# A hidden block's ScalarE chain put off by one product, weight splits held back by a landing time, and idle products at the start, in a two-layer streaming encoder on one core

## The chip, the cores and the metric

The kernel runs on one core of a Trainium2 chip. The core has five engines with instruction queues of their own: TensorE (PE, matrix products, with its weight loads shown as PEld), VectorE (DVE), ScalarE (ACT), GpSimd (POOL) and SyncE (SP, which here issues nearly all transfers). The metric is the device time of one execution in microseconds (us), as the median of several runs.

## What is computed

One step of an encoder with two layers, on 1024 rows of a prompt and 32 rows of a running stream, 1024 features each. Cut to what matters here (rmsnorm is a root mean square norm over the features):

```
for i in (0, 1):
    sh1, sc1, gt1, sh2, sc2, gt2 = split(silu(c) @ w_ada[i] + b_ada[i], 6)
    h = rmsnorm(x, g_norm[i, 0]) * (1 + sc1) + sh1
    mix = sgu_mixer(h)  if i == 0 else  pool_mixer(h)
    x = x + gt1 * rmsnorm(mix, g_norm[i, 1])
    h = rmsnorm(x, g_norm[i, 2]) * (1 + sc2) + sh2
    f = square(relu(h @ w_up[i])) @ w_down[i]        # 1024 -> 4096 -> 1024
    x = x + gt2 * rmsnorm(f, g_norm[i, 3])
```

The mixer of layer 0 is a gated MLP (1024 to 2 x 2048, a 128 x 128 mix of positions, back to 1024); that of layer 1 takes trailing means of 2, 4, 8 and 16 rows and a small product per group. All of it is float32, and the last rows of some intermediate results are outputs too.

## The kernel before

**Tiles.** Activations lie transposed in SBUF, features on the 128 partitions in 8 blocks, rows along the free axis, in three tiles: rows 0 to 383, 384 to 767, and the last 256 with the 32 rows of the running stream.

**Products.** A float32 product is made of three products of a shorter type: each operand is split into a high part (ScalarE writes a rounded copy, names with h: wh, hh, fh) and a low part (VectorE subtracts, names with l: wl, hl, fl), and TensorE adds high times high, low times high and high times low into one PSUM bank. PSUM banks come from three rings: pu (2 banks), pd (3) and pm (3); a ring's next tile waits until the readers of the tile that had the bank are done.

**Weights.** All weights are streamed in one fixed list. `issue` (L463) sends the next load, 512 KB, from SP's queue as soon as one of the few raw buffers is free. `stream_step` takes the next load of the list and issues its split: on ScalarE the high part (L542 for a whole piece, L500 for a part of a quad), on VectorE the low part. The conditioning (w_ada) comes through the same list; VectorE works on it in products of a vector (the tiles aa, line 80 as all operations of its helper) and reduces them (part).

**The order of the work.** The kernel's text is a program in which two clocks are kept by hand while it is written out, `time["pe"]` and `time["dve"]`. `weave` (L765) is called behind each group of products and puts in what fits: a step of the weight stream, if `stream_waits` (L757) doesn't hold it back, and steps of other work (fillers: norms, gates, statistics). A scheduler of the framework then orders the instructions of each engine once more; only the front, in which the order is written out by hand, is kept as it stands (`tc.manual_schedule()`). Each engine executes its instructions in the order that results, so an instruction that waits holds up all behind it on its engine.

**The front** transposes the input rows (xT, L695), makes the first norm (its factor is spread over the partitions by three products with a matrix of ones, pb_h, L850), and the first six conditioning vectors on PE (ada, L583; ScalarE copies the result to adas, L595; two transposes adat, L600, bring it into columns). Then come the products of the gate's v half (pv, L1138), whose operands hh and hl need the norm and the conditioning.

**The channel MLP** runs in passes over its 4096 hidden features; the list `passes` counts them from n = 0. In 14 of them, n = 2 to 8 in layer 0 and n = 15 to 21 in layer 1, tiles 0 and 1 are taken together as a pair (`pair_item`, L1568). A pass has 512 hidden features, in four blocks j, for each tile. Two halves `up(0)` and `up(1)` make two blocks each, in seven products instead of eight, by combinations of the four quarters of the weights (A1, S31, S24, A22, from `quads`) and of the two tiles (combo). Each is a `quad_product` of 12 matmuls of 128 x 128 by 384 columns (L1604 to L1606), in this order of accumulators: pa, pb, pa, pb, pa, pc, pa. The bank of pa goes on accumulating, so ScalarE copies it to SBUF (L1610) at each stage that is used: a1, a2, a3, and pb once, b1. VectorE adds the hidden blocks r12 = a2 + pb, r22 = a3 + b1 and r11 = a1 + pc; r21 is pa at its end. The next product into a bank waits for its copy.

`keep` makes of each hidden block relu (L1578), square (L1579) and a split into a high part (L1326, ScalarE) and a low part (line 80, VectorE). Of a pass's eight blocks the first five go to tiles fh and fl, two to spare tiles that the profile shows as combo_R, and the last to fx. `down` then multiplies them by w_down, 8 blocks of features for each of the two tiles (accumulators pg, three banks, L1066 to L1068), and VectorE adds each to the residual's tile (acc). For the first blocks of the second tile the kernel puts the products of the last hidden block behind the others.

In `up` as it stands, each `keep` is called at once: for instance behind the third use of pa

```
a3 = copy(pa, f"a3{name}")
keep(0, j + 1, add(a3, b1, f"r22{name}"))
weave()
```

Of the kernel before, what the change touches and what calls it, by code (L numbers as in the profile page):

```python
# [11 lines left out]
AF = mybir.ActivationFunctionType  # L12
# [3 lines left out]
P = 128  # L16
# [19 lines left out]
def tile_stream_encoder_step(  # L36
# [26 lines left out]
    act = nc.scalar.activation  # L63
    mm = nc.tensor.matmul
# [3 lines left out]
    time = {"pe": 0.0, "dve": 0.0}  # L68
# [43 lines left out]
    ident = const.tile([P, P], F32, name="ident")  # L112
# [30 lines left out]
    def ps_ms(name):  # L143
        return psum.tile([P, 512], F32, tag="pm", bufs=3, name=name)

    def t_m(name):
        return work.tile([P, 384], F32, tag="m", bufs=3, name=name)
# [21 lines left out]
    one = t_hid("h", "one", F32)  # L169
# [270 lines left out]
            wpos[("up", key[1], key[2] // 2, x)] = wpos[key]  # L440
    raws = {}
    loads = {}
    state = {"issued": 0, "next": 0, "raw": 0, "used": 0, "folds": 0}
    deferred = []

    def in_raw(k):
# [13 lines left out]
    def issue():  # L460
        while state["issued"] < len(stream):
            k = state["issued"]
            kind, key, ap, shape = stream[k]  # L463
            if in_raw(k):
                if state["raw"] == RAW_SLOTS:
                    return
                state["raw"] += 1
                r = t_raw(f"raw{k}")
            elif kind == "x":
                r = x_rows[min(key // 3, NT - 1)]  # L470
                r = r[:, key % 3] if key < 6 else r
            else:
                r = w_tile(f"raw{k}")
            if kind == "x" and key < 6:
                i = nc.sync.dma_start(r, ap.rearrange("t (k n) -> t k n", n=P))
            elif kind == "x":
                for j in range(ap.shape[0] // 32):
                    for a in range(4):
                        i = nc.sync.dma_start(
                            r[32 * a : 32 * a + 32, 4 * (key - 6) + j],  # L480
                            ap[32 * j : 32 * j + 32].rearrange("s (k a m) -> s a k m", a=4, m=32)[:, a],
                        )
            else:
                i = nc.sync.dma_start(r.rearrange("p (a b) -> p a b", a=shape[0]), ap)
            raws[k] = r
            loads[key] = i.ins
            state["issued"] += 1

# [268 lines left out]
    def stream_waits():  # L757

        kind, key = stream[state["next"]][:2]
        if kind in ("w", "one", "two"):  # L760
            return bool(fillers) and wpos[key] > state["used"] + 5 and time["dve"] > time["pe"] + 1.0
        return kind in ("ada", "wide") and time["dve"] > time["pe"] + 0.5
# [52 lines left out]
    def weave(streams=1):  # L815
        if streams:
            n = 0
            run_deferred()
            while n < streams and stream_ready() and not stream_waits():
                stream_step()  # L820
                n += 1
        while time["dve"] < time["pe"] - slack[0] and fillers:
            if not pull():
                break
# [287 lines left out]
    def stream_to(kind, key):  # L1112
        k = max(i for i, s in enumerate(stream) if s[0] == kind and s[1] == key)
        while state["next"] <= k:
            stream_step()
        run_deferred()
# [38 lines left out]
    def fold():  # L1155
        pe_folds.pop(0)()
# [4 lines left out]
    def lo():  # L1161
        late_lo.popleft()()

    def row(h):

        next(h)
        next(h)

    with tc.manual_schedule():
        load_vectors(nc.scalar, 2, slice(0, 2))  # L1170
        issue()
        load_vectors(nc.gpsimd, 0, slice(0, 1))
        load_vectors(nc.gpsimd, 1, slice(0, 1))
        load_vectors(nc.gpsimd, 2, slice(2, 4))
        bring(AF.Silu)
        stream_to("x", 0)
        turn_conditions()
        stream_to("x", 2)
        bring(AF.Sqrt)
        next(h0)  # L1180
        next(h0)
        stream_to("ada", (0, 4, 0))
        turn_vectors()
        stream_to("ada", (0, 4, 1))
        next(h0)
        statistics(h0)
        fold()
        next(h0)
        stream_to("ada", (0, 0, 1))
        fold()  # L1190
        stream_to("w", ("v", 0, 0))
        next(h0)
        late_hi.pop()()
        next(h0)
        lo()
        early_mm((0, 1, 2), 0)
        stream_to("x", 5)
        next(h1)
        turn()
        next(h1)  # L1200
        stream_to("ada", (0, 5, 1))
        turn()
        fold()
        next(h1)
        statistics(h1)
        turn()
        early_ps.extend(ps_up(f"pv0_{b}") for b in (3, 4))
        next(h1)
        row(h1)
        stream_to("ada", (0, 1, 1))  # L1210
        next(h0)
        early_mm((3,), 0)
        fold()
        early_mm((4,), 0)
        for q in range(1, 4):
            stream_to("w", ("v", 0, q))
            row(h0)
            lo()
            next(h1)
            row(h1)  # L1220
            if q == 3:
                stream_to("w", ("v", 1, 0))
            early_mm((0, 1), q)
            if q < 3:
                conditions(q + 1)
                fold()
                next(h0)
            early_mm((2,), q)
            if q < 3:
                fold()  # L1230
            early_mm((3, 4), q)
        bring(AF.Gelu_apprx_tanh)
        ps = ps_ms("pv0_5")
        v_mm(ps, 0, 5, range(KB))
        early_end((0,))
        stream_to("w", ("v", 1, 1))
        early_end((1, 2))
        stream_to("w", ("v", 1, 2))
        early_end((3,))
        stream_to("w", ("v", 1, 3))  # L1240
        early_end((4,))
        v_end(ps, 0, 5)
# [40 lines left out]
    for p, b in v_order:  # L1283
        ps = ps_dn(f"pv{p}_{b}")
# [29 lines left out]
    fillers.append(("state", sgu_state()))  # L1314

    fold_lag[0] = 0.3


    pending = []
# [249 lines left out]
    def pair_item(p, after, ends):  # L1569
# [3 lines left out]
        made = [0]  # L1573

        def keep(t, j, r, src=None):
            if src is None:
                src = r
            act(out=r, in_=src, func=AF.Relu)  # L1578
            act(out=r, in_=r, func=AF.Square)  # L1579
            name = f"{l}_{c}_{t}_{j}"  # L1580
            if made[0] < 5:
                a, b = t_hid("h", "fh" + name), t_hid("l", "fl" + name)
            elif made[0] < 7:
                a, b = spare_hid[made[0] - 5]
            else:
                x = work.tile([P, 768], F32R, tag="x3", bufs=3, name="fx" + name)
                a, b = x[:, :n], x[:, n:]
            made[0] += 1
            split(a, b, r, n)
            hid[t][j] = a, b  # L1590
# [17 lines left out]
        def copy(ps, name):  # L1608
            x = t_c(name)
            act(out=x, in_=ps[:, :n], func=AF.Copy)  # L1610
            return x

        def add(a, b, name):
            r = t_m(name)
            tt(out=r, in0=a[:, :n], in1=b[:, :n], op=ALU.add)
            return r

        def up(jp):
            name = f"{l}_{c}_{jp}"
            j = 2 * jp  # L1620

            def done(key):
                w_finish(("up", p, jp, key))

            pa, pb = ps_ms(f"pfa{name}"), ps_up(f"pfb{name}")
            quad_product(pa, jp, ("A1", 0), -11, True)
            a1 = copy(pa, f"a1{name}")
            weave()
            if jp == 0:
                flush()  # L1630
                finish("combos")
            quad_product(pb, jp, ("S31", 512), 1, True)
            b1 = copy(pb, f"b1{name}")
            weave()
            quad_product(pa, jp, ("S24", 0), 2, False)
            a2 = copy(pa, f"a2{name}")
            weave()
            quad_product(pb, jp, ("S24", 512), -22, False)
            done("S24")
            keep(0, j, add(a2, pb, f"r12{name}"))  # L1640
            weave()
            quad_product(pa, jp, ("S31", 0), 3, False)
            done("S31")
            a3 = copy(pa, f"a3{name}")
            keep(0, j + 1, add(a3, b1, f"r22{name}"))
            weave()
            pc = ps_up(f"pfc{name}")
            quad_product(pc, jp, ("A1", 512), -21, True)
            done("A1")
            keep(1, j, add(a1, pc, f"r11{name}"))  # L1650
            weave()
            quad_product(pa, jp, ("A22", 0), 4, False)
            done("A22")
            keep(1, j + 1, t_m(f"r21{name}"), pa[:, :n])
            weave()

        def term(wh, wl, t, j, d):
# [28 lines left out]
        slack[0] = 2.0 if l == 1 else 0.0  # L1686
        up(0)
        up(1)
        if passes[p + 1][2] != PAIR:
            slack[0] = 0.0  # L1690
            finish(f"ffn{l}_{NT - 1}")
            fillers.append(late_norm.pop())
# [474 lines left out]
```

## Time and profile before

| | us |
|---|---|
| median of 3 runs | 2106.13 |
| the three runs | 2105.29, 2106.66, 2106.13 |
| the profiled execution | 2106.9 |
| its span in the profile | 2105.1 |
| the TensorE clock granted, mean over the span | 0.998 of full |

The span goes from the first to the last instruction that the profiler recorded; the profiled execution's time has 1.8 us beside it. A row of the profile names engine, line, operation and tiles (output <- inputs, buffer numbers left out); in a timeline it begins with start and duration in us, rows of one kind that follow each other are put together with a count, and the brackets hold the idle time of the engine before the row and what ended it. A tile's name in a row is that of its buffer's current use. A matmul's duration holds its way through the array: matmuls overlap, and their rate is seen from their starts.

### The profile page before, as it was taken

How to read it: one execution, taken by the hardware profiler on the slowest of the kernel's cores; microseconds unless marked ns; L12 is line 12 of the kernel's file. 1: busy time of each engine (PE TensorE's matmuls, PEld its weight loads, DVE VectorE, ACT ScalarE, POOL GpSimd, SP SyncE). 2: the span in 40 equal slices, each digit the busy share in tenths (PEclk: the TensorE clock that was granted, in tenths of full speed). 3: DMA queues.
4: the chain of work that ended last, by engine and by line, in shares of the span. 5: the costliest groups of instructions: out<-in, count | busy, mean ns of one | idle time of the engine just before them, and what ended most of it. 6: DMA issues, size and time to landing. Idle time of an engine off the chain costs nothing.

```text
span 2105.1 us, 32717 instructions
## 1 busy us (share of the span) xinstructions
PE 2084.7 (99%) x12786; PEld 2013.1 (96%) x12786; DVE 1569.3 (75%) x2811; ACT 1034.3 (49%) x1853; POOL 22.3 (1%) x44
## 2 busy tenths in 40 slices
PE   8999999999999999999999999999999999999998
PEld 6878999999999999999999999999999999999998
DVE  6788737556869988888767989897868654579554
ACT  5634322234447644344446766776435443365555
POOL 0000000000000000000000000000000000001100
PEclk9999999999999999999999999999999999999999
DMA  8586524243524443443334667643223221148862
GB/s 295 159 268 213 187 79 135 85 150 106 159 70 156 130 126 113 128 126 115 114 96 130 207 198 238 192 140 106 92 76 109 88 80 52 54 125 233 202 180 93
DMA packets 397040, 294.98 MB, mean 140 GB/s; under 512 B 46638, under 2 KB 360278, under 8 KB 396884
## 3 DMA queue, kind: packets, MB, share of 16 engines
q1 hardware_dynamic: 395956, 291.60, 45.8%
q8 instruction: 100, 1.64, 0.3%
q0 software_dynamic: 896, 1.28, 0.2%
q14 instruction: 56, 0.46, 0.1%
q10 hardware_dynamic: 32, 0.01, 0.0%
HBM read 262.18 MB, written 30.66 MB: 139 GB/s over the span
## 4 chain that ended last, share of the span: by engine, by line
PE 89%; DVE 6%; ACT 2%; DMA 2%; issue 1%; SPq 0%; DVEq 0%; ACTq 0%
PE pg L1067 11%; PE pg L1066 11%; PE pg L1068 11%; PE pf L1066 4%; PE pf L1068 4%; PE pf L1067 4%; PE po L1066 3%; PE po L1067 3%; PE po L1068 3%; PE pfa L1604 3%; PE pfa L1606 3%; PE pfa L1605 3%; PE pu L1066 3%; PE pu L1068 3%; PE pu L1067 3%; PE pv L1092 2%
## 5 line engine op out<-in xcount | busy, mean ns | idle before, releaser
L1066 PE MATMUL pg<-fh,wh_dn 128*128 128x384 f32 (+1 forms) x960 | 311.2, 325 | 0.1
L1067 PE MATMUL pg<-fl,wh_dn 128*128 128x384 f32 (+1 forms) x960 | 310.8, 324 | 0.0
L1068 PE MATMUL pg<-fh,wl_dn 128*128 128x384 f32 (+1 forms) x960 | 310.0, 323 | 0.0
L80 DVE TENSOR_TENSOR acc<-acc,pg 128x384 f32<-128x384 f32 (+1 forms) x272 | 144.7, 533 | 111.9 <-PE pg L1068 110.7
L80 DVE TENSOR_TENSOR wl_dn<-raw,wh_dn 128x1024 fp32r<-128x1024 f32 x136 | 166.2, 1223 | 70.0 <-ACT wh_dn L542 36.7
L80 DVE SCALAR_TENSOR_TENSOR aa<-raw,csil,aa 128x512 f32<-128x512 f32 (+1 forms) x364 | 207.9, 621 | 13.0 <-DMA raw<-in_w_ada_dram 12.9
L1066 PE MATMUL pf<-hh,wh_up 128*128 128x288 f32 (+1 forms) x640 | 195.4, 305 | 0.4 <-ACT wh_up L542 0.4
L1067 PE MATMUL pf<-hl,wh_up 128*128 128x288 f32 (+1 forms) x640 | 194.0, 303 | 0.0
L1068 PE MATMUL pf<-hh,wl_up 128*128 128x288 f32 (+1 forms) x640 | 193.7, 303 | 0.0
L542 ACT ACTIVATE wh_dn<-raw 128x1024 fp32r<-128x1024 f32 x136 | 143.8, 1057 | 88.7 <-PE pf L1067 33.8
L1066 PEld LDWEIGHTS pg<-fh,wh_dn 128*128 128x128 f32 x960 | 180.2, 188 | 1.4 <-ACT fh L1326 1.0
L1067 PEld LDWEIGHTS pg<-fl,wh_dn 128*128 128x128 f32 x960 | 180.3, 188 | 0.9 <-DVE fl L80 0.4
L1068 PEld LDWEIGHTS pg<-fh,wl_dn 128*128 128x128 f32 x960 | 180.2, 188 | 0.0
L542 ACT ACTIVATE wh_up<-raw 128x1024 fp32r<-128x1024 f32 x80 | 84.7, 1059 | 80.3 <-PE pg L1067 44.9
L1066 PEld LDWEIGHTS pf<-hh,wh_up 128*128 128x128 f32 x640 | 120.1, 188 | 1.1 <-ACT wh_up L542 0.7
L80 DVE TENSOR_TENSOR wl_up<-raw,wh_up 128x1024 fp32r<-128x1024 f32 x80 | 97.6, 1221 | 31.0 <-ACT wh_up L542 30.5
L1068 PEld LDWEIGHTS pf<-hh,wl_up 128*128 128x128 f32 x640 | 120.5, 188 | 0.3 <-DVE wl_up L80 0.3
L1067 PEld LDWEIGHTS pf<-hl,wh_up 128*128 128x128 f32 x640 | 120.2, 188 | 0.4
L80 DVE TENSOR_TENSOR wl_up_S<-raw,wh_up_S 128x512 fp32r<-128x512 f32 (+1 forms) x84 | 71.9, 866 | 55.8 <-PE pfb L1605 51.5
L1066 PE MATMUL pg<-fx,wh_dn 128*128 128x288 f32 (+1 forms) x352 | 109.4, 311 | 0.4 <-ACT fx L1326 0.4
L1067 PE MATMUL pg<-fx,wh_dn 128*128 128x288 f32 (+1 forms) x352 | 108.3, 308 | 0.0
L1068 PE MATMUL pg<-fx,wl_dn 128*128 128x288 f32 (+1 forms) x352 | 108.2, 307 | 0.0
(400 smaller groups left out, 5549.5 us busy)
## 6 DMA issues: line engine op xcount, KB each, us to landing
raw<-in_ffn_w_up_dram SPq DMA_DIRECT2D x136, 512.0 KB, 4.1
raw<-in_ffn_w_down_dram SPq DMA_DIRECT2D x136, 512.0 KB, 3.9
raw<-in_w_ada_dram SPq DMA_DIRECT2D x90, 512.0 KB, 4.3
raw<-in_sgu_w_in_dram SPq DMA_DIRECT2D x40, 512.0 KB, 4.0
xd<-acc SPq DMA_DIRECT2D x8, 1536.0 KB, 8.3
raw<-in_sgu_w_out_dram SPq DMA_DIRECT2D x24, 512.0 KB, 3.8
xo_r<-xd SPq DMA_DIRECT2D x32, 384.0 KB, 4.1
vd<-vt SPq DMA_DIRECT2D x32, 256.0 KB, 3.6
```

The costliest lines, as they stand in the source:

```text
L80: return op(out, *args, **kw)
L542: act(out=wh, in_=r, func=AF.Copy)
L1066: mm(ps[:, :n], wh, rh, start=i == 0, stop=False)
L1067: mm(ps[:, :n], wh, rl, start=False, stop=False)
L1068: mm(ps[:, :n], wl, rh, start=False, stop=i == last)
L1092: mm(ps[:m, :], a_h, wh[:, o : o + 512], start=k == 0, stop=False)
L1604: mm(ps[:, :n], wh[:, o], rh, start=first and k == 0, stop=False, skip_group_check=True)
L1605: mm(ps[:, :n], wh[:, o], rl, start=False, stop=False, skip_group_check=True)
L1606: mm(ps[:, :n], wl[:, o], rh, start=False, stop=k == HK - 1, skip_group_check=True)
```

## The change

Three parts, all in how the program is written out; no product of the reference is added or left out.

1. In `pair_item`, the calls of `keep` go into a queue `later`, and `settle(n)` carries out the oldest until n are left. r12's chain is issued behind the copy a3, r22's and r11's behind the products that follow them, r21's of the first half behind the second half's copy a1; behind `up(1)` the rest is settled. The tile of r21 is allocated inside `keep`.
2. `issue` notes for each load when it should have landed: 4.2 us behind the later of the two clocks at its issue. From the end of the v stage on (`wary`), `stream_waits` holds a stream step back while the PE clock is before that time, unless its weights are wanted among the next two.
3. In the front, `keep_clock(4)` multiplies the identity by itself four times into an unused bank, once ahead of the transposes adat of the first conditioning vector and once behind them.

```diff
@@ state
+    landed = {}
-    state = {"issued": 0, "next": 0, "raw": 0, "used": 0, "folds": 0}
+    state = {"wary": False, "issued": 0, "next": 0, "raw": 0, "used": 0, "folds": 0}
@@ issue
             raws[k] = r
+            landed[k] = max(time["pe"], time["dve"]) + 4.2
@@ stream_waits
         kind, key = stream[state["next"]][:2]
+        near = kind in ("w", "one", "two") and wpos[key] <= state["used"] + 2
+        if state["wary"] and not near and time["pe"] < landed.get(state["next"], 1e9):
+            return True
@@ front
+    def keep_clock(n):
+        ps = ps_ms("idle")
+        for _ in range(n):
+            mm(ps[:, :P], ident, ident, start=True, stop=True)
...
         stream_to("ada", (0, 0, 1))
+        keep_clock(4)
         fold()
+        keep_clock(4)
         stream_to("w", ("v", 0, 0))
@@ ahead of the passes
     fold_lag[0] = 0.3
+    state["wary"] = True
@@ pair_item, keep
-            if src is None:
-                src = r
-            act(out=r, in_=src, func=AF.Relu)
+            if r is None:
+                r = t_m(f"r21{l}_{c}_{j}")
+            act(out=r, in_=r if src is None else src, func=AF.Relu)
@@ pair_item, up
+        later = deque()
+        def settle(n):
+            while len(later) > n:
+                keep(*later.popleft())
...
             a1 = copy(pa, f"a1{name}")
+            settle(0)
             weave()
...
-            keep(0, j, add(a2, pb, f"r12{name}"))
+            later.append((0, j, add(a2, pb, f"r12{name}")))
...
             a3 = copy(pa, f"a3{name}")
-            keep(0, j + 1, add(a3, b1, f"r22{name}"))
+            settle(0)
+            later.append((0, j + 1, add(a3, b1, f"r22{name}")))
...
-            keep(1, j, add(a1, pc, f"r11{name}"))
+            later.append((1, j, add(a1, pc, f"r11{name}")))
+            settle(1)
...
-            keep(1, j + 1, t_m(f"r21{name}"), pa[:, :n])
+            later.append((1, j + 1, None, pa[:, :n]))
+            settle(1)
@@ pair_item, its end
         up(1)
+        settle(0)
```

## The prediction

> **What bounds the kernel now.** I read the page first, then the waits of PE, then the clock by stretches of the front, and last the timeline around each wait of a pair pass. The page's share of busy time and its chain:
>
> ```profile
> PE 2084.7 (99%) x12786; PEld 2013.1 (96%) x12786; DVE 1569.3 (75%) x2811; ACT 1034.3 (49%) x1853; POOL 22.3 (1%) x44
> ...
> PE 89%; DVE 6%; ACT 2%; DMA 2%; issue 1%; SPq 0%; DVEq 0%; ACTq 0%
> ```
>
> PE is busy for 2084.7 of 2105.1 us, and the chain that ended last is PE for 89%. So PE sets the time, and the change, which takes away no useful matmul, can gain only what PE loses: idle time, and time at a lowered clock. The waits of PE give the first:
>
> ```profile
> PE pv L1138 <- ACT hh L1026: 1.8, 2, 1.1
> PE pfb L1604 <- ACT b L1610: 1.5, 4, 0.5
> PE pfa L1604 <- ACT a L1610: 1.4, 2, 0.7
> ```
>
> The columns are total us, times, longest. The second and third row are what the first part of the change is aimed at: in a pair pass PE waits for ScalarE to copy an accumulator out of its bank, 2.9 us in six waits. The first row lies in the front. There the other loss lies too:
>
> ```profile
> 10.37:13.78 3.41, 2.58 (x27) 1.48 (x19) 1.59 (x9) 1.60 (x6) 0.00 (x0) 1.00 1.09 401
> 13.78:17.20 3.42, 1.75 (x21) 0.78 (x19) 2.23 (x9) 2.19 (x5) 0.00 (x0) 1.00 1.02 387
> 17.20:20.61 3.41, 3.41 (x8) 2.36 (x9) 2.19 (x3) 3.35 (x7) 0.00 (x0) 0.50 1.07 378
> 20.61:24.02 3.41, 3.41 (x24) 2.75 (x22) 1.18 (x6) 1.01 (x3) 0.00 (x0) 1.00 1.09 390
> ```
>
> Each row is a stretch of the front: its length, the busy us of PE, PEld, DVE, ACT and POOL, then the granted PE clock. The clock is 0.50 in one stretch alone, the one behind that in which PE was busy for 1.75 of 3.42 us (51%). The stretch with 2.58 of 3.41 us (76%) is followed by full clock.
>
> **The change, part by part.** *Part 1: idle matmuls in the front.* Two blocks of four 128x128 products on the identity, ahead of and behind the two transposes adat. PE in that place, by the timeline (start, us, engine, line, operation, count, and in brackets the idle time before it and who ended it; one row of ScalarE is among them):
>
> ```profile
> 12.78 0.94 PE L850 MATMUL pb_h<-r_h,ones 128*128 128x128 f32 x6
> 13.75 0.49 ACT L1044 ACTIVATE r_h<-pb_h 128x384 f32<-128x384 f32 x1 [0.42 <-PE pb_h L850]
> ...
> 15.49 0.44 PE L600 MATMUL adat<-ident,adas 128*128 128x128 f32 x2 [0.56 <-ACT adas L595]
> 17.04 0.68 PE L1138 MATMUL pv<-wh_v,hh 128*128 128x512 f32 x1 [1.11 <-ACT hh L1026]
> ...
> 18.29 0.63 PE L1138 MATMUL pv<-wh_v,hh 128*128 128x512 f32 x1
> 18.72 0.63 PE L1138 MATMUL pv<-wh_v,hl 128*128 128x512 f32 x1
> ...
> 20.98 0.40 PE L1138 MATMUL pv<-wh_v,hl 128*128 128x512 f32 x1
> 21.21 0.39 PE L1138 MATMUL pv<-wh_v,hh 128*128 128x512 f32 x1
> ...
> 23.03 1.03 PE L695 MATMUL xT<-ident,x_rows 128*128 128x128 f32 x8
> ```
>
> Price: pb_h is written as three fp32 products and stands as six instructions in 0.94 us, about 0.11 us apart once the 0.28 of the last one's drain is taken off; so four idle products are eight such instructions, 0.9 us a block. Cover: PE idles 0.56 us ahead of adat and 1.11 ahead of pv. The first block can also start while the last product before it drains, about 0.2 us sooner, so it overlaps the first gap by all but some 0.1 to 0.2 us: adat, and the mod and hh behind it, come +0.1 later. The second block (0.9) fits its 1.11. Nothing else waits behind them on PE: the bank that the first block takes was last read by the copy of pb_h, which ends at 14.24.
>
> Gain: PE in the stretch 13.78 to 17.20 becomes 1.75 + 0.9 + 0.9 = 3.5 less overlap, near the whole stretch, far over the 76% after which the clock was kept. At half clock the pv products start 0.43 us apart (18.29, 18.72), at full clock 0.23 (20.98, 21.21). Some eight start between 17.2 and 20.6; 8 x 0.20 = 1.6 us, of which 0.1 goes where the second must wait for its own operand (hl). With the +0.1, the front ends **1.4 us** earlier. Bounds: +0.1 (clock drops all the same) and -1.6.
>
> Does it reach the end? The chain behind the pv group is PE for its own sake, product after product; the loads that it needs in the next 20 us were issued on SP, which this part doesn't touch, and are not what it waits for: behind xT no row of PE's waits names a load. A pair pass's waits on loads start from PE events too (a buffer that PE frees), so they move along. I take all of it through.
>
> [...]
>
> *Part 2: the chain taken one product later.* In before, ScalarE runs relu, square and split of a hidden block before the next accumulator copy. The instruction order of the two kernels, set side by side (it isn't a time), says what a scheduler makes of it: the same multiset of instructions on DVE and ACT, all queues of SP and POOL in the same order, no difference at all before the first pair pass (about 705 us), and few places moved in each pass. The two longest waits and one of the four b waits:
>
> ```profile
> 782.51 1.06 ACT L542 ACTIVATE wh_dn<-raw 128x1024 fp32r<-128x1024 f32 x1 [1.98 <-DMA raw<-in_ffn_w_down_dram]
> 783.48 0.47 ACT L1610 ACTIVATE a<-pfa 128x384 f32<-128x384 f32 x1
> 784.00 0.44 PE L1604 MATMUL pfa<-combo_R,wh_up_S 128*128 128x384 f32 x1 [0.70 <-ACT a L1610]
> ...
> 844.34 1.06 ACT L542 ACTIVATE wh_dn<-raw 128x1024 fp32r<-128x1024 f32 x1 [1.74 <-DMA raw<-in_ffn_w_down_dram]
> 845.31 0.47 ACT L1610 ACTIVATE b<-pfb 128x384 f32<-128x384 f32 x1
> 845.83 0.44 PE L1604 MATMUL pfb<-hh,wh_up_S 128*128 128x384 f32 x1 [0.51 <-ACT b L1610]
> ```
>
> ScalarE wasn't busy with a chain here: it stood 1.98 and 1.74 us on a load, in the split wh_dn, and the copy sat behind that split. In the new order the copy b of passes n = 4 to 7 and the copy a of n = 3 still stand right behind the same split. So these five waits stay: **0**. What the order does move, pass by pass (n counts passes as the kernel's list does):
>
> n = 2: copy a of the second half, ahead of the split before, now stands behind it.
>
> ```profile
> 717.96 0.49 ACT L1610 ACTIVATE a<-pfa 128x384 f32<-128x384 f32 x1 [1.57 <-PE pfa L1606]
> 718.68 1.06 ACT L542 ACTIVATE wh_dn<-raw 128x1024 fp32r<-128x1024 f32 x1 [0.23 <-DMA raw<-in_ffn_w_down_dram]
> 719.84 0.33 PE L1604 MATMUL pfa<-combo_R,wh_up_S 128*128 128x384 f32 x1
> ...
> 726.56 0.51 DVE L80 TENSOR_TENSOR combo_R<-r,combo_R 128x384 fp32r<-128x384 f32 x1
> 727.00 1.26 DVE L644 TENSOR_REDUCE part<-raw 128x16 f32<-128x512 f32 x2
> 727.81 0.33 PE L1067 MATMUL pg<-combo_R,wh_dn 128*128 128x384 f32 x1
> ```
>
> The split ends at 719.74, the copy at 720.2, PE wants the bank at 719.84: +0.4. The low part combo_R goes behind the two reduces and an add of about 0.5, so it ends near 728.8 instead of 727.07, while PE wants it at 727.81, or four matmuls (0.7) later where the new order puts them: +0.3. Less a little where a chain no longer precedes a copy, **+0.6** for n = 2 (0 to +0.9).
>
> n = 3: the low part fx goes behind three more aa products, and PE's use of it comes nine matmuls earlier.
>
> ```profile
> 793.72 0.55 DVE L80 TENSOR_TENSOR fx<-r,fx 128x384 fp32r<-128x384 f32 x1
> 795.80 2.07 DVE L80 SCALAR_TENSOR_TENSOR aa<-raw,csil,aa 128x512 f32<-128x512 f32 x3
> 798.25 0.34 PE L1066 MATMUL pg<-fx,wh_dn 128*128 128x384 f32 x1
> ```
>
> Use: 798.25 - 9 x 0.17 = 796.7; the low part, one matmul later, 796.9. Ready: from the place of the add ahead of it (0.5 before 793.72), four aa (0.7 each), the other low part and fx (0.5 each), 793.2 + 3.8 = 797.0. The accumulator add behind it, 797.5, frees the bank that PE wants at 797.2 to 797.3. So 0.1 to 0.3, and a restart of 0.1 each: **+0.4** (0 to +0.9).
>
> n = 16: copy a goes two instructions forward.
>
> ```profile
> 1519.40 0.93 ACT L1326 ACTIVATE fh<-r 128x384 fp32r<-128x384 f32 x2
> 1520.23 1.05 ACT L542 ACTIVATE wh_dn<-raw 128x1024 fp32r<-128x1024 f32 x1
> 1521.18 0.47 ACT L1610 ACTIVATE a<-pfa 128x384 f32<-128x384 f32 x1
> 1521.70 0.44 PE L1604 MATMUL pfa<-combo_R,wh_up_S 128*128 128x384 f32 x1 [0.68 <-ACT a L1610]
> ```
>
> Two splits fh are 0.93; the wait is 0.68. If the weight split also starts sooner, all goes; if it waits for its load, little: **-0.4** (-0.8 to +0.4). n = 17 and 18: a short stall each; **-0.2** (-0.4 to +0.2). Sum of part 2: +0.6 + 0.4 - 0.4 - 0.2 = **+0.4** (-1.2 to +2.4).
>
> *Part 3: splits held back until 4.2 us behind their issue* (the model's clock). Held-back splits show in the same order; they add no wait on the chip, since a split waits for its load's semaphore as before. It costs and gains nothing beyond part 2.
>
> Sum: -1.4 + 0.4 = -1.0. The profiled execution took 2106.9 us (span 2105.1 and 1.8 around it), so 2105.9; it lies 0.8 over the median of the three runs, 2106.13, so that the forecast for the median is **2105.1**.
>
> **The rivals.** *B: the front gains nothing.* [...] For it: one profile can't tell. Against: a 51% stretch is the only one followed by half clock. Time: 2106.1 + 0.4 + 0.1 = 2106.6.
>
> *C: the change does what it says*, every copy of an accumulator in a pair pass free of waits: the 2.9 us of the two rows and, for six restarts, 0.1 each (0.44 against 0.33 of a matmul), with the front, and with none of the costs of n = 2 and 3. 2106.1 - 1.4 - 3.5 = 2101.2. Against: the order of the instructions, and the 1.98 and 1.74 us on a load.
>
> *D: slower.* A hidden block's chain comes one product, twelve matmuls of 0.17, so 2.1 us, later, and the first blocks of down want it. In layer 0 there is slack: fx is ready at 794.3 and wanted at 798.25, 4.0 us. In layer 1 there is none:
>
> ```profile
> 1533.87 0.34 PE L1068 MATMUL pg<-fh,wl_dn 128*128 128x384 f32 x1
> 1534.23 0.44 PE L1067 MATMUL pg<-combo_R,wh_dn 128*128 128x384 f32 x1
> ```
>
> This step is 0.36 instead of 0.17 and the next begins 0.1 late: 0.3. If each of the 14 pair passes lost that, +4.2: with the rest 2105.1 + 4.2 = 2109.3. It decides from the point at which the slack falls under 2.1 us; against it, PE's order follows the chain (the matmuls of a late block are put behind others), and after the last product nothing is put off.
>
> **How the numbers follow.** The forecast (front gains, part 2 small) 0.52; B 0.26; C 0.07; D 0.10; a disturbance of the load order that I don't see, either way, 0.05. Part 2's bounds around the forecast give 2103.5 to 2107.1, around B 2105.0 to 2108.6. The range **2102.4 to 2108.6** holds the forecast and B with these bounds, reaches half way to C, and leaves out C itself and most of D. 0.2% is 4.2 us, about what a measurement of this kernel can tell from no change; so faster (under 2101.9) is C and a little, 0.08; slower (over 2110.3) is D's upper half, 0.07; same 0.85.
>
> **What would show it.** Part 1: sixteen idle instructions, the stretch 17.2 to 20.6 at clock 1.00, xT (23.03 before) starting near 21.6; wrong if a stretch at 0.50 remains. Part 2: the waits pfb <- b still 1.5 in four, at the same passes; pfa <- a a new wait near 720 less 1.4, and that of 1521.70 shorter; fx of n = 3 waited for. If the row pfb <- b is gone, C was right; if down products wait on fx, fh or combo_R in many passes, D. A change of more than 4 us in either direction would make the prediction wrong in kind.

## The result, and the profile after

| | before | changed |
|---|---|---|
| median of 13 runs, us | 2106.13 (2104.92 to 2109.71) | 2111.22 (2109.18 to 2113.82) |
| ratio | | 1.0023, 95% interval 1.0014 to 1.0031 |
| span of the profiled execution | 2105.1 | 2109.6 |

The change costs 4.8 us by the ratio (0.0023 x 2106; the medians lie 5.1 apart); the forecast was a gain of 1.0, and the range ended at 2108.6. The profile shows 4.5 of it, so it can be read for the cause. First the waits of TensorE in the changed kernel (total us, times, longest):

```profile
PE pfb L1618 <- ACT b L1624: 3.5, 4, 2.1
PE psp L1434 <- DMA vl<-vd: 2.0, 1, 2.0
PE pv L1143 <- ACT hh L1031: 0.9, 2, 0.7
...
PE pfa L1618 <- ACT a L1624: 0.9, 2, 0.7
PE pg L1071 <- ACT fx L1340: 0.7, 1, 0.7
```

The second row is new: psp is the product of the gate stage that mixes positions, and it waits 2.0 us for a load of the normalised v rows (vl). In before it waited 0.6, for VectorE:

```profile
PE psp L1420 <- DVE aa L80: 0.6, 1, 0.6
```

The stage has nothing of the change in it. The clock by stretches, in the front and in the gate stage of the changed kernel (length, busy us of PE, PEld, DVE, ACT, POOL, then the clock):

```profile
13.78:17.20 3.42, 3.42 (x38) 2.62 (x36) 2.06 (x8) 1.70 (x4) 0.00 (x0) 1.00 1.04 423
17.20:20.61 3.41, 3.04 (x13) 2.17 (x12) 2.38 (x3) 3.38 (x7) 0.00 (x0) 1.00 1.06 380
...
248.70:252.20 3.50, 1.48 (x11) 1.19 (x10) 3.50 (x7) 0.00 (x0) 0.00 (x0) 0.97 0.67 187
252.20:255.60 3.40, 3.40 (x15) 3.40 (x14) 3.34 (x8) 0.90 (x3) 0.30 (x1) 0.52 0.85 289
```

The front does what was foretold: PE is busy through 13.78 to 17.20, and the next stretch keeps its clock. But the wait of psp leaves PE busy for 1.48 of 3.50 us at 248.7, and behind it the clock is down to 0.52: the stretch at half clock that the front has lost stands again 235 us later.

The times of the same VectorE and ScalarE instructions, subtracted, say where the 4.5 us come from (changed less before; the median of each stretch, which the reader can't see in one view): 0.8 ahead from 25 to 155 us, 0.1 ahead at 170 to 200, 0.4 behind at 230, 0.5 at 260, 1.5 behind from 300 to 690; 2.2 behind at 835 and 3.6 at 850; 4.8 at 1060, 5.4 at 1230; 4.1 at 1525, 4.5 from 1700 to the end. So 0.7 goes near 160 us (a second profile of before, e3 below, loses 0.6 there against this one, so that isn't the change's), 1.6 in the gate stage, some 3 in the pair passes of layer 0, 0.7 near 1215, and layer 1 gives one back.

What delays vl? The chain of waits of the changed kernel through that stage (start, us, what):

```profile
222.26 5.05 DMA raw<-in_sgu_w_out_dram
227.34 1.07 ACT wh_o L544
228.43 1.23 DVE wl_o L80
230.12 0.58 DVE wr L80 x3
...
245.89 2.36 DMA out_dram<-vst
248.32 2.85 DMA vl<-vd
251.30 2.25 PE psp L1434 x12
```

It goes from one load of weights over ScalarE into a long train of VectorE work, and from there over SP's queue to vl. In before the chain through this place is PE's own products up to 227.7 us and the train of VectorE work behind them; the load isn't in it. In the changed kernel that one load took 5.05 us. The transfers around it in both kernels, from the load's issue to its landing (q1 carries data, q8 the instructions; the last column of an issue is us to landing), before first:

```profile
q1 hardware_dynamic: 542, 0.80, 62.7%
...
raw<-in_sgu_w_out_dram SPq DMA_DIRECT2D x1, 512.0 KB, 3.4
```

and changed:

```profile
q1 hardware_dynamic: 804, 1.17, 73.1%
q8 instruction: 1, 0.02, 1.4%
...
raw<-in_sgu_w_out_dram SPq DMA_DIRECT2D x1, 512.0 KB, 5.1
```

In before no instruction transfer falls into this load, in the changed kernel one does. That led to the theory that the experiments try. The page counts for queue q8, in both kernels:

```profile
q8 instruction: 100, 1.64, 0.3%
```

100 transfers of 16 KB for 25,572 instructions of PE and PEld (12,786 each): one for 256 instructions in the mean. The 16 idle matmuls with their weight loads are 32 more instructions, so each later fetch comes 32 instructions sooner against the work. By the trace's records of q8 the fetch in question, the ninth, began at 229.02 us in before and at 224.69 in the changed kernel, behind 2,199 and 2,191 instructions of PE and PEld; the last of the 100 began behind 25,414 to 25,429 in all 13 profiles of this document. So these fetches keep to TensorE's count of instructions and not to the time, and are read here as fetches of its code. The load into which the ninth fell in the changed kernel took 5.1 us instead of 3.4.

### The profile page after: what moved, and what is told of

The parts are those of the page before. It is cut to its first block, busy times and chain, and to the rows that moved or that the text cites. A ratio compares the mean times of both kernels' runs of the same rounds, so it can differ in the third digit from the quotient of the medians.

```text
span 2109.6 us, 32751 instructions
## 1 busy us (share of the span) xinstructions
PE 2086.5 (99%) x12802; PEld 2015.6 (96%) x12802; DVE 1569.2 (74%) x2811; ACT 1037.2 (49%) x1853; POOL 22.4 (1%) x44
## 4 chain that ended last, share of the span: by engine, by line
PE 88%; DVE 5%; DMA 3%; ACT 2%; issue 1%; DVEq 0%; SPq 0%; ACTq 0%
PE pg L1072 11%; PE pg L1071 11%; PE pg L1073 11%; PE pf L1071 4%; PE pf L1073 4%; PE pf L1072 4%; PE po L1071 3%; PE po L1073 3%; PE po L1072 3%; PE pfa L1618 3%; PE pfa L1620 3%; PE pfa L1619 3%; PE pu L1071 3%; PE pu L1073 3%; PE pu L1072 3%; PE pv L1097 2%
## 5 line engine op out<-in xcount | busy, mean ns | idle before, releaser
L80 DVE TENSOR_TENSOR wl_dn<-raw,wh_dn 128x1024 fp32r<-128x1024 f32 x136 | 166.4, 1224 | 67.2 <-ACT wh_dn L544 36.5
L544 ACT ACTIVATE wh_up<-raw 128x1024 fp32r<-128x1024 f32 x80 | 84.8, 1060 | 79.9 <-PE pg L1072 45.6
```

Source lines behind the costliest of these rows:

```text
L80: return op(out, *args, **kw)
L544: act(out=wh, in_=r, func=AF.Copy)
```

## The experiments

Each run is compared with runs of before on the same chip. The first four tell the parts of the change apart; they still went by two other theories: 1, the loss sits in the pair passes; 2, TensorE's earlier start is given back in the gate stage. The theory "code" was formed on their traces: the added instructions shift TensorE's code fetches, and a fetch that falls into a load on which the work waits makes it 1.2 to 1.7 us longer (sgu_w_out took 4.8 and 5.1 us with one in it, 3.4 to 3.6 without). Its rivals from e5 on: "place" (the idle products disturb by where they stand) and "count" (each instruction more costs). The landing time (part 3 of the prediction) was not run by itself. In the traces the changed kernel, its idle products aside, has PE's, SP's and GpSimd's instructions in the order of e2, which lacks this part.

**e1, the front alone.**

```diff
         stream_to("ada", (0, 0, 1))
+        keep_clock(4)
         fold()
+        keep_clock(4)
```

> The kernel before with the idle products of the front alone; all other instructions stand in the same order on every engine. Theory 1 (the front's gain is kept, and the loss sits in the pair passes): 0.8 to 1.4 us faster than before. Theory 2 (TensorE's earlier start is given back in the gate stage, where it then waits for a load of the gate's v rows and loses a stretch at half clock): the same as before or up to 1.5 us slower, with a stretch at clock 0.50 near 242 us and a wait of psp on vl of about 2 us in the profile.

2113.97 against 2107.50: ratio 1.0032 (1.0019 to 1.0044), 6.5 us slower, more than either theory gave, and more than the whole change. Its waits:

```profile
PE psp L1428 <- DMA vl<-vd: 2.8, 1, 2.8
...
PE pp L1987 <- DMA wg<-in_pool_w_grp_dram: 1.2, 1, 1.2
```

The wait of psp is there, and the stretch at half clock behind it; the load of sgu_w_out took 5.1 us with a fetch in it. A second wait is new: pp, a product of the pool mixer near 1550 us, waits for its weights wg.

**e2, the moved chain alone** (the changed pair_item, without keep_clock and with `wary` never set).

> The chain put off by one product alone, without idle products and without the landing time. Theory 1: 5.5 to 6.5 us slower than before (the 4.9 of the changed kernel and the front's gain on top). Theory 2: 3.0 to 4.0 us slower, with the stretch at 0.50 near 17 to 21 us as in before and none near 242. In both, the waits of pfb on the copy b grow at pass n = 4 and a new wait of pfa at n = 2 stands near 721.

2106.96 against 2107.50: ratio 0.9997 (0.9988 to 1.0006). Both theories missed: the moved chain costs nothing that can be measured. Its waits on copies:

```profile
PE pfb L1609 <- ACT b L1615: 1.4, 3, 0.6
PE psp L1425 <- DMA vl<-vd: 1.1, 1, 1.1
...
PE pfa L1609 <- ACT a L1615: 0.6, 1, 0.6
```

**e3 and e4, second profiles of both kernels.**

> The kernel before once more, for a second profile. What differs between its two profiles is no effect of the change. If the wait of psp on vl and the clock in the gate stage (0.74 us lost and full clock in the first profile) are the same again, theory 2 has a steady ground to stand on; if psp waits 2 us here too, that wait is chance.

> The changed kernel once more, for a second profile. Theory 2 expects the 2.0 us of psp on vl and the half clock near 242 again. If the 2.1 us wait for the copy b at pass n = 4 and its load of 6.4 us are chance of the first profile, they are about 0.6 and 4.9 here.

In before (2106.02), psp waited 1.1, sgu_w_out took 3.6, and the front kept its clock, without idle products. In the changed kernel (2109.74):

```profile
PE psp L1434 <- DMA vl<-vd: 3.6, 1, 3.6
PE pfb L1618 <- ACT b L1624: 1.6, 4, 0.6
```

psp waits again, sgu_w_out takes 4.8 us again: no accident. There was no stretch at half clock behind it this time. The 2.1 us of the copy b at 850 us don't come in every execution: here the longest is 0.6. In e5 below it is 1.8 there again. Where it came, in the first profile and in e5, a load of w_ada just ahead took 6.5 and 6.2 us; what lengthened that load stays open.

**e5, e6, e7: the same instructions in another place, and in another number.**

```diff
+    def pad(n):
+        ps = ps_ms("pad")
+        for _ in range(n):
+            mm(ps[:32, :1], ones[:, :32], ones[:, :1], start=True, stop=True)
     with tc.manual_schedule():
+        pad(8)        # e5; e6: pad(16); e7: pad(8), and the idle products of the front
```

> The kernel before with eight tiny float32 products (32 columns of weights, 1 column of data, 16 matmul instructions and as many weight loads, the same count as the idle products of the front) at its very start, where TensorE waits for the first rows until 4.2 us; no idle products later. Theory 'code': the 32 instructions move every later fetch of TensorE's code (16 KB in one transfer, 256 instructions) some 4 us forward against the work, into the load of sgu_w_out issued near 222 us, and into the load wg near 1550; so 5 to 6.5 us slower than before, as the front alone (6.5) less its own 0.3, with psp waiting 2 us or more on vl. Theory 'place' (the idle products disturb by where they stand, in the front): same as before within 1 us.

2114.68 against 2107.18: ratio 1.0034 (1.0022 to 1.0047), 7.5 us slower (by the medians; 5 to 6.5 were foretold), though the products stand where PE has nothing to do. Waits, and the transfers around the load of sgu_w_out:

```profile
PE psp L1427 <- DMA vl<-vd: 2.7, 1, 2.7
...
PE pp L1986 <- DMA wg<-in_pool_w_grp_dram: 1.6, 1, 1.6
```

```profile
q8 instruction: 1, 0.02, 1.6%
...
raw<-in_sgu_w_out_dram SPq DMA_DIRECT2D x1, 512.0 KB, 5.1
```

The same two loads are hit, and the same two waits stand there. "Place" falls.

> The same with sixteen tiny products (32 matmul instructions, 64 instructions in all). Theory 'code': the fetch near 229 us moves to about 220.5, ahead of the load it hit, and the one near 1547 to about 1540, ahead of the load wg; so within 1.5 us of before, with psp waiting about 1 us on vl, as in before. Theory 'count' (more instructions on TensorE are slower, each): 10 us or more over before. Theory 'place': the same as before.

2109.40: ratio 1.0011 (1.0002 to 1.0020). Twice the instructions cost a third of the time, so "count" falls. Waits, and the load:

```profile
PE pg L1066 <- ACT fx L1333: 1.6, 1, 1.6
PE psp L1427 <- DMA vl<-vd: 1.1, 1, 1.1
```

```profile
raw<-in_sgu_w_out_dram SPq DMA_DIRECT2D x1, 512.0 KB, 3.6
```

sgu_w_out and wg are free, as foretold; it still lost 2.2, since the fetch now fell into the train of loads near 1216 us (xo_r took 4.9 us instead of 3.7 and fx came 1.6 late). "Within 1.5 us" missed that.

> The idle products of the front as in the change (16 matmul instructions) and eight tiny ones at the start (16 more), so that the count is that of the run before this one. Theory 'code': within 1.5 us of before, the clock of the front kept at 1.00 in the profile. Theory 'place': 6.5 us slower, as the front alone.

2109.32: ratio 1.0013 (1.0004 to 1.0021). The idle products of the front are in, and yet the time is e6's, not e1's (2.1 over before, again more than the 1.5 foretold). Its clock in the front was kept, psp waited 0.7, and the wait of fx near 1224 was 2.0.

**e8, e10: fewer instructions for the same end.** In e8 each block of the front is one product of the identity with 384 columns of activations, in e10 `keep_clock(2)` stands for `keep_clock(4)` in the changed kernel.

> The two blocks of the front kept, but each as one float32 product of the identity with 384 columns of activations: 4 matmul instructions in all instead of 16, PE busy for about 1.3 us instead of 1.8. Theory 'code': the fetch near 229 moves 1 us only and misses the load; so 0 to 1.5 us faster than before (the clock of the front, where before lost it), psp waiting about 1 us. Theory 'place': 5 us or more slower.

> The changed kernel with two idle products in each of the two blocks instead of four (8 matmul instructions in all, 16 with their weight loads). Theory 'code': the fetch near 229 moves by half as much, to about 227, behind the load of sgu_w_out (3.5 us, not 5.1), and may hit the load of w_ada issued near 228 as in the run with wide products, which lost 2; so 1 to 3 us over before, less than the changed kernel. The clock of the front is kept (PE busy for some 78% of the stretch). Theory 'place': half of the loss of the front alone, 3 us, with the load of sgu_w_out as slow as in the changed kernel.

e8: 2109.73, ratio 1.0009 (1.0000 to 1.0018); e10: 2109.39 against 2107.58, ratio 1.0008 (0.9999 to 1.0017). In both sgu_w_out took 3.6, but psp waited 2.2 and 1.7, and in e8 the stretch at half clock stands behind that wait. In both the fetch (at 227.63 and 226.81) fell into another load of the stage, one of w_ada, which the chain of waits shows in the place of sgu_w_out, first e8, then e10:

```profile
223.76 6.71 DMA raw<-in_w_ada_dram
```

```profile
223.92 6.36 DMA raw<-in_w_ada_dram
```

By its landings this load took 5.0 to 5.4 us in before, e2, e3, e6, e7 and e9, and VectorE stood idle ahead of the product that takes it, for 1.0 us in e8 and 0.7 in e10. e8 was slower than the code theory had given it, which had looked at sgu_w_out alone; e10 was as it gave.

**e9: the same instructions behind the gate stage.** `pad(8)` at the head of the first pair pass; it comes to stand among the products of the first pass.

> The kernel before with the eight tiny products (16 matmul instructions) among the products of the first pass of the channel MLP, behind the gate stage and ahead of the pair passes; nothing else moves. Theory 'code': up to 600 us nothing changes, so psp waits about 1 us on vl and no stretch at half clock stands near 242; behind it the fetches are moved as in the run with the same count at the start, so the transfer xo_r near 1215 and the load wg near 1548 are hit again, 1.5 to 4 us over before in all (that run lost 7.5, some 3 of it in the gate stage). Rival (sixteen instructions more in any place cost 6 to 7 us): 2113.

2110.64 against 2107.58: ratio 1.0013 (1.0004 to 1.0022), 2.7 by the ratio. The gate stage is as in before, the losses begin behind it:

```profile
PE psp L1426 <- DMA vl<-vd: 1.0, 1, 1.0
...
PE pp L1987 <- DMA wg<-in_pool_w_grp_dram: 0.7, 1, 0.7
```

and the transfers from the issue of xo_r to its landing:

```profile
q8 instruction: 1, 0.02, 1.2%
...
xo_r<-xd SPq DMA_DIRECT2D x1, 384.0 KB, 5.1
```

**e11: the changed kernel with `pad(12)`**, 40 matmuls more in all, chosen so that the fetches miss all three loads.

> The changed kernel as it is, with twelve tiny float32 products at its start: 24 matmul instructions more, 40 with the idle products of the front. By the places that the runs so far gave (the fetch near the load of sgu_w_out at +6.0 us behind its issue with none, +2.4 with 16, -0.4 with 32; near xo_r at +5.2, +2.6 and +1.1 to 0.4) the fetch then lies about 1.8 us ahead of sgu_w_out, 0.5 ahead of xo_r and 3 ahead of wg, and hits none of the three. Theory 'code': 2.5 to 5 us faster than the changed kernel, so from 1.5 under before to 1.5 over it, with psp waiting about 1 us, sgu_w_out 3.6 us and xo_r 3.7 us. Rival (the idle products and the moved chain are slow by themselves): 4.9 us over before or more.

2111.12 against 2107.30: ratio 1.0016 (1.0007 to 1.0025), 1.5 to 5.3 us: the forecast of a time failed. The run by itself doesn't exclude its rival either (4.9 or more, for idle products and a moved chain that are slow by themselves); against that stand e2, where the moved chain costs nothing, and e7, where the idle products are in for 2.1. Its waits:

```profile
PE pg L1071 <- ACT fx L1347: 2.0, 1, 2.0
PE psp L1441 <- DMA vl<-vd: 1.5, 1, 1.5
```

The transfers between 1213.2 and 1217.3 us:

```profile
q8 instruction: 1, 0.02, 1.9%
...
raw<-in_ffn_w_down_dram SPq DMA_DIRECT2D x1, 512.0 KB, 4.4
wg<-in_pool_w_grp_dram SPq DMA_DIRECT2D x1, 256.0 KB, 4.6
```

sgu_w_out (3.6) and the wg near 1550 (2.7) were missed, as meant. The fetch at 1214.2 was ahead of xo_r, but in the two loads issued just before it (the last two rows), and xo_r, behind them in the same queue, took 5.6. Behind the wait of fx stands a stretch at half clock:

```profile
1223.50:1226.90 3.40, 1.49 (x11) 1.48 (x12) 3.35 (x5) 1.86 (x4) 0.00 (x0) 1.00 0.99 355
1226.90:1230.30 3.40, 3.40 (x17) 3.40 (x16) 2.57 (x5) 2.14 (x3) 0.00 (x0) 0.50 1.00 281
```

By the subtracted times, against the profile of before, e11 is 1.3 us behind at 1180 and 4.9 at 1300: 3.6 of the 4.2 of its profile are lost at this train of loads. In e6 it is 1.6 of 2.2. To miss one load isn't enough where loads follow each other closely.

**All profiles together.** Columns: the start of the fetch, counted from the issue of the load, and the load's us; the wait of psp.

| run | PE matmuls added ahead | fetch, sgu_w_out | load | psp waits | fetch, xo_r | load |
|---|---|---|---|---|---|---|
| before | 0 | +6.0 | 3.4 | 0.6 | +5.3 | 4.0 |
| e3 (before) | 0 | +6.2 | 3.6 | 1.1 | +5.2 | 3.7 |
| e2 | 0 | +6.3 | 3.5 | 1.1 | +4.6 | 3.6 |
| e9 | 0, then 16 | +6.2 | 3.7 | 1.0 | +2.3 | 5.1 |
| e8 | 4 | +5.4 | 3.6 | 2.2 | +4.0 | 3.8 |
| e10 | 8 | +4.4 | 3.6 | 1.7 | +2.8 | 3.6 |
| changed | 16 | +2.4 | 5.1 | 2.0 | +2.0 | 4.8 |
| e4 (changed) | 16 | +2.5 | 4.8 | 3.6 | +2.7 | 4.8 |
| e1 | 16 | +2.2 | 5.1 | 2.8 | +2.6 | 5.4 |
| e5 | 16 | +2.4 | 5.1 | 2.7 | +2.0 | 4.8 |
| e6 | 32 | -0.4 | 3.6 | 1.1 | +1.1 | 4.9 |
| e7 | 32 | -0.4 | 3.6 | 0.7 | +0.4 | 5.2 |
| e11 | 40 | -3.1 | 3.6 | 1.5 | -2.1 | 5.6 |

A fetch that starts 0.4 to 2.7 us behind a load's issue goes with a load of 4.8 to 5.4 us (four of four for sgu_w_out, seven of seven for xo_r); every other load but the last is at 3.4 to 4.0. These bounds are read off this table: in e10 a fetch 2.75 behind the issue left xo_r at 3.6, where one at 2.68 (e4) went with 4.8. The load wg near 1550 took 3.9, 4.3 and 3.4 us with a fetch 1.4, 1.8 and 0.9 behind its issue (e1, e5, e9) and 2.6 to 2.8 in the others; in the changed kernel its fetch fell 5.3 behind, which is one reason why it lost less than the front alone.

Two more readings of the same traces, which no view shows as such. First, all loads of weights (512 KB), each against the same load in those of the 13 profiles in which no fetch began between 0.5 us ahead of its issue and 4 us behind it: with a fetch 2.0 to 2.7 us behind the issue (47 loads) the load was 0.8 us longer in the mean, and over 0.8 longer in 25 of them; with none near, in 34 of 3,191. With a fetch 0.4 to 1.2 us behind it was 0.3 longer (164 loads). So it isn't the loads of the table alone that are longer; they are among the hardest hit. Second, the traces have 16 updates of the semaphore for the landing of such a load. For sgu_w_out the 15th of them came 3.4 to 3.7 us behind the issue in all 13 profiles. The 16th came at most 0.2 later in the nine without a fetch in the load, and 1.3 to 1.6 later in the four with one. So in these four one update of the 16 came late, and the load had landed only with that one.

## Why the prediction was wrong

- **That PE sets the time and the useful work is unchanged** held: PE busy went from 2084.7 to 2086.5 us, the idle products among it.
- **Part 1, the clock** (the parts are numbered here as in the prediction: the idle products, the moved chain, the landing time), held in the profile: PE was busy for 3.42 of 3.42 us, and the next stretch kept clock 1.00, where before it was 1.75 of 3.42 and then 0.50. PE in the front by the timeline of the changed kernel:

```profile
15.08 1.16 PE L1173 MATMUL idle<-ident 128*128 128x128 f32 x8
16.07 0.38 PE L602 MATMUL adat<-ident,adas 128*128 128x128 f32 x2
...
17.56 0.50 PE L1143 MATMUL pv<-wh_v,hh 128*128 128x512 f32 x1 [0.22 <-ACT hh L1031]
...
22.23 1.03 PE L697 MATMUL xT<-ident,x_rows 128*128 128x128 f32 x8
```

  From pv to xT it took 4.7 us (22.23 - 17.56) instead of 6.0 (23.03 - 17.04): 1.3 of the 1.5 worked out. The cost of the first block was mis-sized: from the transposes adat of the vector before (13.76; 13.55 in before) to this adat it took 2.31 instead of 1.94, so 0.4 and not 0.1. And the rest of this profile's front is 0.2 late for its loads. Net 0.8 there, not 1.4.
- **Rival B** was half of the truth: of six profiles without idle products in the front three kept the clock (e2, e3, e9) and three didn't (before, e5, e6), of seven with them all seven did. When it was given its chance, no run had shown yet that the loss stays away in some executions; e3 showed it: with PE busy for 1.75 of 3.42 us between 13.78 and 17.20, as in before, the clock stayed at 1.00. So the gain, on the mean, is half of 1.3 less 0.4: some 0.3 us, an estimate from these counts.
- **"I take all of it through"** is the step that failed, with the cost of the idle products beside it. The step looked only at what the idle products do in time. It looked at the loads of the next 20 us and let those of the pair passes move along with PE, and left out that the products are instructions: 32 more in TensorE's code, by which the later fetches of code move (the ninth from 229.02 to 224.69 us), some of them into loads on which the work waits (sgu_w_out, 5.1 us instead of 3.4). No term of the sum had this; the front alone cost 6.5 us. The row of q8 stood on the page of before, 100 transfers, 0.3% of the engines' time, and the prediction passed over it. That behind xT no row of PE's waits names a load was true of one profile: in e3, the same kernel, psp waits 1.1 us for vl. The chain through the gate stage could have warned too: from 228 us on it isn't PE there but a train of VectorE work, and at its end PE waited for VectorE by 0.6 us already.
- **Part 2** agrees with its bounds as far as the time can tell: +0.4 (-1.2 to +2.4) forecast, -0.6 measured (0.9988 to 1.0006 of 2107.5: -2.5 to +1.3), an interval as wide as the bounds. Its terms, from the timeline of the changed kernel:

```profile
720.25 1.07 ACT L544 ACTIVATE wh_dn<-raw 128x1024 fp32r<-128x1024 f32 x1 [2.34 <-DMA raw<-in_ffn_w_down_dram]
721.22 0.47 ACT L1624 ACTIVATE a<-pfa 128x384 f32<-128x384 f32 x1
721.75 0.45 PE L1618 MATMUL pfa<-combo_R,wh_up_S 128*128 128x384 f32 x1 [0.20 <-ACT a L1624]
...
798.80 0.44 PE L1072 MATMUL pg<-fx,wh_dn 128*128 128x384 f32 x1 [0.18 <-DVE fx L80]
```

  At n = 2 the copy a stands behind the split and its load, and PE starts 0.54 behind its last matmul (721.21) instead of 0.17: 0.4 as forecast; the low part combo_R made no stall, though 0.3 was put down for it. At n = 3 fx is late by 0.35 (798.28 to 798.80 is 0.52), forecast 0.4. At n = 16 the wait of 0.68 is gone from the changed kernel and from e2, the better end of its bounds. The five waits behind weight splits stayed, as said: four for b (first table of waits) and one of 0.7 for a.
- **Rivals C and D** didn't come: the copies still wait for loads, and no down product waits in many passes. The slower side came by a way that none of the rivals held. Nearest is the 0.05 put on a disturbance of the loads that wasn't seen; but it is the lengths of the loads that changed, and SP's order is the same.
- **Part 3** was not measured by itself. PE and SP run the order of e2, which lacks it, so nothing shows that it costs or gains.

What stays open: why e11 waits 1.5 us for vl though no fetch falls into the loads of that stage (its load of w_ada there took 5.9 us); what the 0.5 to 3 us in the pair passes of layer 0 are made of in the runs with added products, in which two profiles of one kernel differ by 1.4 (e2 and e3, without any, are 1.2 and 0.7 later there against the same profile of before); and why the last update of sgu_w_out comes 1.3 to 1.6 us late when the fetch took 0.9 to 1.4. No version beat the kernel before: e2 can't be told from it.

## What to carry to other kernels

Instructions without a cost in their own place cost here by being instructions: 16 matmuls and their weight loads, put where TensorE had nothing to do, moved the fetches of its code into loads on which the work waited (sgu_w_out, 5.1 us instead of 3.4; wg near 1550, 4.3 us instead of 2.6 to 2.8), and the kernel was 7.5 us slower (e5). So when a small edit moves the time by more than its own work, compare the durations of the loads in both traces, and look for an instruction transfer inside those that grew; then add the same number of harmless instructions where the engine idles, and if the time moves as much, the edit itself wasn't the cause. And a chain that is PE for 89% says nothing of the stage in which it isn't, here the gate stage from 228 us on.

## What the runs showed of the hardware

- TensorE's code was fetched in 100 transfers of 16 KB, one for 256 of its 25,572 instructions in the mean; the one near the load of sgu_w_out took 0.9 to 1.4 us, and in the four profiles in which it fell into that load of 512 KB, the load took 4.8 to 5.1 us instead of 3.4 to 3.7: 15 of its 16 updates came within 3.4 to 3.7 us, the last 1.3 to 1.6 later.
- PE waiting for 2.0 to 2.8 us (busy 1.48 of 3.50 in the changed kernel, 0.78 of 3.50 in e1) was followed by a stretch of 3.4 us at half clock in five profiles (changed, e1, e5, e8; e11 behind fx), but not behind 2.0 us in e7 nor 3.6 us in e4.
- A float32 product of 128 x 128 by 128 columns stands as two matmuls, 0.11 us apart in pb_h; eight such matmuls on the identity took 1.16 us, the last one's 0.28 among it.
